# Probabilities of two slots transposed into one tile of two PSUM banks, and one bank for all other transposes

## The chip, the cores and the metric

The kernel runs on one core of one Trainium2 chip. The metric is the device time of one execution in microseconds. Before the change three runs gave a median of 1200.68 us (1199.81 to 1203.39). In the profile PE is TensorE's matmul side and PEld its weight loads, DVE is VectorE, ACT is ScalarE, POOL is GpSimd, SP issues DMAs.

## What is computed

The reference is one layer of a decoder trunk on x of 1 x 1024 x 1024 in float32. The part that matters here is the attention of one block of 128 queries, done for eight blocks, two groups of four heads and two branches (selected keys and a window):

```python
s_s = jnp.einsum('bghqd,bgqkld->bghqkl', qi, kg)
...
p_s = masked_softmax(s_s.reshape(flat_shape),
                     m_s.reshape(bsz, B_KV, 1, Q_BLOCK, k_top * L_SEL)).reshape(s_s.shape)
o_s = jnp.einsum('bghqkl,bgqkld->bghqd', p_s.astype(vg.dtype), vg)
...
s_w = jnp.einsum('bghqd,bgkd->bghqk', qi, kwi)
...
p_w = masked_softmax(s_w, m_w)
o_w = jnp.einsum('bghqk,bgkd->bghqd', p_w.astype(vwi.dtype), vwi)

o = (gi[..., 0:1] * o_c.astype(jnp.float32) + gi[..., 1:2] * o_s.astype(jnp.float32)
     + gi[..., 2:3] * o_w.astype(jnp.float32))
```

Ahead of it stand a norm and the products with w_in (z), beside it the gMLP heads, behind it W_o with a residual, a mixture of 16 experts, a gated projection and a last norm.

## The kernel before

Every float32 product is made of three products of float32r parts: each operand is split into hi (what float32r holds) and lo (the rest), by a copy on ACT and a subtraction on DVE. The kernel runs in stages: z in column chunks (to about 230 us), the attention (239 to 614 us), the last block's way out and the routing (614 to 660), the experts (660 to 1080) and the gated projection (1080 to the end).

The attention takes the query blocks in the order 1, 2, 3, 4, 0, 5, 6, 7. A unit is one block of queries, one group and one branch; a slot is one block of 128 keys of one unit, and there are 132 slots. In slot s the program writes, in this order:

- `trans(s + 1)`: four PE transposes (L643) of the next slot's probabilities P into one PSUM bank `tp`, then the copy `ph` on ACT (L649) and the subtraction `pl` on DVE (L651, written a little later);
- what `later` put off to this slot: the exponentials of a bank of scores one slot after its maxima (L579), then the factors f and the scaling of P by f on POOL (L603), which must be over before that P is transposed;
- the output of a finished unit (L688), and a step of `prep` for a block to come (its queries transposed at L476, scores over the compressed keys S at L482 and L486, their probabilities Pc transposed at L510);
- products that fill (`work`): first of u (L264, 7 in a slot), then of W_o (L770, 3 in a slot), for whose operands `trans4` transposes four tiles (L754);
- one or two banks of scores S (L564, with masks at L566 and L568), followed by their maxima on DVE (L569);
- `mult(s)`: the two products O with ph (L668) and pl (L669); where a unit pair begins, two more with Pc (L662, L663).

The program does not run in that order. A scheduler takes each instruction when its operands and buffers are free by the scheduler's own model of time, earlier written first, and so fixes one order for each engine; the fill has a lower priority (-100000) and may not go ahead of the last transposes written before it. The engines then run their queues strictly in that order, so an instruction at the head of a queue that waits holds up all behind it.

PSUM has eight banks, and in the attention they are: `tp` three (shared in turn by all transposes: L643, L476, L510, L688, L754), S two, O one, and two for the fill. Tiles `ph` and `pl` have three buffers each. `due` holds the slot in which a bank of scores is written at the latest.

Of the kernel before, what the change touches and what calls it, by code (L numbers as in the profile page):

```python
# [34 lines left out]
# columns of the packed constants (shape-only) and of the packed small parameters  # L35
# [8 lines left out]
# columns of w_in, in the order in which they are multiplied  # L44
# [7 lines left out]
class Slots:  # L52
    """Tiles by name from one pool, or in turn from several."""
# [18 lines left out]
class K:  # L72
# [3 lines left out]
    # hi = the part of (src * scale) that float32r holds, lo = the rest of it  # L76
# [41 lines left out]
    # the rotary embedding of z [128, n, 64]  # L118
# [11 lines left out]
    # a chunk of w_in's columns with the norm's gain, hi and lo  # L130
# [16 lines left out]
    # half of two tiles of x, transposed, hi and lo  # L147
# [10 lines left out]
    # the factor of a tile's norm  # L158
# [64 lines left out]
    # the parts of u's way out: each waits for the one before  # L223
    def evac_u(self, tt, p):
# [12 lines left out]
        def two():  # L237
# [3 lines left out]
            # gelu by tanh, whose table holds exp too; the half of it is in what u is multiplied with  # L241
# [16 lines left out]
    # the products of tiles with a chunk, one at a time  # L258
# [38 lines left out]
    def extras(self):  # L297
# [5 lines left out]
        # the mixing weights of the gMLP heads: w_sT[s, h, t] is kept where t >= s  # L303
# [10 lines left out]
    # the gMLP heads mix within chunks of 128 tokens: four tiles of v  # L314
# [18 lines left out]
    # compressed keys (transposed, hi over lo) and values (hi | lo, zero outside their group)  # L333
# [46 lines left out]
    # work that is due some slots on: k slots from now, at the slot's start  # L380
# [10 lines left out]
    # a slot without attention  # L391
# [6 lines left out]
    # Attention of the query blocks in order, a slot being one block of 128 keys of one unit (query  # L398
    # block, group, branch) in the product with the values. A slot holds the scores of units that
    # follow, the transposed probabilities of the next slot, and other products (work).  # L400
    def attention(self, blocks, done, work, count):
# [19 lines left out]
        # where a chunk's probabilities go: the place whose last use is done first  # L421
# [13 lines left out]
        # the heads whose scores share a bank, in order, with the slots in which they are due  # L435
# [5 lines left out]
        for b, (c, _, _) in enumerate(banks):  # L441
            u = chunks[c][0]
            n = len(u["cs"])
            u0 = start[c - chunks[c][1]]
            due.append(u0 - (7 if n == 2 else 5) - (u["banks"][-1] - b))
# [4 lines left out]
        # a bank for scores; what reads the one before it in the same place goes first  # L450
# [6 lines left out]
        # The four heads of a group, transposed: hi over lo, and lo over hi; then the softmax over  # L457
        # the compressed keys of both groups, transposed and split.
        def prep(i):
# [31 lines left out]
            # laid out as [q, head in group, group, key], so that one transpose serves both groups  # L491
# [25 lines left out]
        # The steps of prep: when they are due (before the block's first slot), and which banks and  # L517
        # slots have to come first, as the tiles are those of the block before.
# [23 lines left out]
        # scores of some heads and a chunk; their probabilities follow  # L542
# [43 lines left out]
        # whether the queries for it are ready, or can be  # L586
# [4 lines left out]
        # probabilities times the gate over the sum  # L591
        def stats(u):
# [18 lines left out]
            # the chunks' sums at the maximum of both  # L611
# [17 lines left out]
        # a unit's probabilities, complete  # L629
# [7 lines left out]
        # the probabilities of a block of keys, transposed  # L637
        def trans(s):
            c, u, k, kb = slots[s]
            ensure(u)  # L640
            tp = ps.tile([128, 4, 128], F32, name="tp")
            for h in range(4):
                anchor[0] = PE.transpose(tp[:, h], u["P"][k][:, h, kb * 128:(kb + 1) * 128], self.idf)  # L643
            if kb == u["cs"][k][1] - 1:
                state["transposed"] = c + 1
            ph = sb.tile([128, 512], F32R, name="ph")
            pl = sb.tile([128, 512], F32R, name="pl")
            v = tp.rearrange("p h q -> p (h q)")
            AC.activation(ph, v, AF.Copy)  # L649
            parts[s] = ph, pl  # L650
            return lambda: V.tensor_sub(pl, v, raw(ph))  # L651
# [49 lines left out]
        trans(0)()  # L701
        yield
        for s in range(len(slots)):
            self.now = s
            lo = trans(s + 1) if s + 1 < len(slots) else None
            self.run_later()
            if lo:
                lo()
# [25 lines left out]
    # W_o with the norms' gains: loads (c, columns' half) run ahead of the splits  # L734
# [22 lines left out]
    # 512 columns, transposed, hi and lo  # L757
# [6 lines left out]
    # the products of a half with W_o, one at a time  # L764
# [8 lines left out]
    # The products that fill the slots of the attention: u of the last four tiles, then W_o of the  # L773
    # blocks that are done, the residual, and the experts' input with its router logits.
    def work(self, W, blocks):
# [63 lines left out]
        for n, i in enumerate(blocks[:-1]):  # L839
# [16 lines left out]
            for k in range(2):  # L856
                yield from self.prod(p[k], X["tob"], 1, k, False, True)
                add(X, k, p[k])
                if k == 0:
                    trans_h(X, 0)  # L860
                else:
                    rest(X, N)
        # the last query block's part that doesn't wait for its attention
        X = M[blocks[-1]]
        for k in range(2):
            s = slice(k * 512, (k + 1) * 512)
# [1021 lines left out]
```

## Time and profile before

| | us |
|---|---|
| median of three runs | 1200.68 |
| span of the profiled execution | 1201.4 |
| attention, 239.3 to 614.3 | 375.0 |
| PE busy in the whole span | 1127.4 (94%) |
| DVE, ACT, POOL busy in the span | 772.5, 676.6, 573.0 |

A row of the view of groups gives the line, the engine, the operation with its output and input, how many there are, their busy time and the mean length of one. A matmul's length is not the time that it holds PE for, as matmuls overlap: that is the distance from one start to the next in the timeline. "PEclk" is the granted TensorE clock as a share of the full one (1.00 is 2.4 GHz, 0.50 is 1.2 GHz).

### The profile page before, as it was taken

To read this page: it belongs to the slowest core of one execution; us is meant where nothing else is said; L and a number is where in the kernel's file an instruction comes from. 1 tells how busy PE (TensorE), PEld (TensorE's weight loads), DVE (VectorE), ACT (ScalarE), POOL (GpSimd) and SP (SyncE) were. 2 spreads that over 40 slices of the span, in tenths; PEclk is the share of its full clock that TensorE was granted. 3 is DMA by queue.
4 is the path that set the end of the run, shared out by engine and by line. 5 is a ranking of instruction groups with operands and counts; after the bars stand their busy time and mean duration, and the time that the engine had idled before them with its cause. 6 is when DMAs were issued, how large, how long until landed. Compare 5 with 4: busy or idle time off the path is not lost. (4 is left out here: it accounts for less than half of the span.)

```text
span 1201.4 us, 17857 instructions
## 1 busy us (share of the span) xinstructions
PE 1127.4 (94%) x5993; PEld 866.5 (72%) x5993; DVE 772.5 (64%) x1207; ACT 676.6 (56%) x1306; POOL 573.0 (48%) x639
## 2 busy tenths in 40 slices
PE   7999999899999999999996799999999999959996
PEld 5798778687788888887873566677666766635886
DVE  4461245467876787767649867698657875636764
ACT  6652155467667777666633456667565756435433
POOL 1461342467544343434324776578556865322542
PEclk9999999999899999999998899999999999989999
DMA  8685243412432120231176498997899976465561
GB/s 273 199 215 134 72 127 90 138 58 88 179 105 69 47 97 19 80 115 49 66 280 240 157 340 306 344 370 292 309 320 322 333 251 199 126 249 190 175 220 70
DMA packets 75849, 219.66 MB, mean 183 GB/s; under 512 B 12776, under 2 KB 20328, under 8 KB 71136
## 3 DMA queue, kind: packets, MB, share of 16 engines
q1 hardware_dynamic: 63200, 177.68, 42.9%
q0 software_dynamic: 7792, 27.77, 7.5%
q10 hardware_dynamic: 4752, 12.93, 2.8%
q8 instruction: 52, 0.85, 0.3%
q14 instruction: 53, 0.43, 0.1%
HBM read 247.44 MB, written 40.11 MB: 239 GB/s over the span
## 5 line engine op out<-in xcount | busy, mean ns | idle before, releaser
L1407 DVE TENSOR_TENSOR wl<-ra,wh 128x1024 fp32r<-128x1024 f32 x128 | 218.8, 1727 | 62.1 <-ACT wh L1406 48.3
L1407 POOL TENSOR_TENSOR wl<-ra,wh 128x1024 fp32r<-128x1024 f32 x64 | 171.3, 2678 | 120.2 <-ACT wh L1406 105.0
L1406 ACT ACTIVATE wh<-ra 128x1024 fp32r<-128x1024 f32 x176 | 180.8, 1057 | 77.1 <-PE y L90 44.0
L264 PE MATMUL z<-w,xh 128*128 128x512 f32 (+1 forms) x576 | 170.9, 378 | 7.8 <-ACT w L83 7.5
L603 POOL TENSOR_SCALAR P<-P,f 128x384 f32<-128x384 f32 (+3 forms) x188 | 105.6, 585 | 104.7 <-DVE f L624 61.8
L579 ACT ACTIVATE P<-S,nm 128x256 f32<-128x256 f32 (+3 forms) x192 | 105.5, 556 | 49.3 <-DVE nm L569 45.6
L264 PEld LDWEIGHTS z<-w,xh 128*128 128x128 f32 x576 | 104.9, 190 | 27.1 <-ACT w L83 7.5
L90 PE MATMUL gu<-wh,mxl 128*128 128x512 f32 x272 | 109.3, 402 | 11.2 <-DVE mxl L81 11.2
L89 PE MATMUL gu<-wl,mxh 128*128 128x512 f32 x272 | 109.4, 402 | 8.7 <-DVE wl L1407 7.9
L88 PE MATMUL gu<-wh,mxh 128*128 128x512 f32 x272 | 114.5, 421 | 0.8 <-ACT mxh L80 0.8
L651 DVE TENSOR_TENSOR pl<-tp,ph 128x512 fp32r<-128x512 f32 x132 | 89.8, 685 | 39.0 <-ACT ph L649 38.4
L569 DVE TENSOR_REDUCE nm<-S 128x1 f32<-128x384 f32 (+3 forms) x148 | 91.6, 627 | 31.5 <-PE S L568 18.9
L264 PE MATMUL z<-w,xl 128*128 128x512 f32 (+1 forms) x288 | 108.6, 378 | 1.2 <-DVE xl L81 1.2
L649 ACT ACTIVATE ph<-tp 128x512 fp32r<-128x512 f32 x132 | 78.3, 601 | 42.0 <-PE tp L643 41.4
L564 PE MATMUL S<-kT,qT 128*128 128x384 f32 (+3 forms) x384 | 92.7, 350 | 7.7 <-ACT P L579 5.6
L770 PE MATMUL wo<-wo,th 128*128 128x512 f32 x256 | 90.1, 425 | 0.0
L643 PE MATMUL tp<-c,P 128*128 128x128 f32 x528 | 84.0, 277 | 0.6 <-POOL P L603 0.6
L564 PEld LDWEIGHTS S<-kT,qT 128*128 128x128 f32 x384 | 63.1, 196 | 17.2 <-ACT P L579 7.9
L643 PEld LDWEIGHTS tp<-c,P 128*128 128x128 f32 x528 | 65.7, 143 | 12.6 <-POOL P L603 0.9
L88 PEld LDWEIGHTS gu<-wh,mxh 128*128 128x128 f32 x272 | 52.2, 192 | 23.8 <-ACT wh L1406 7.5
L90 PEld LDWEIGHTS gu<-wh,mxl 128*128 128x128 f32 x272 | 51.9, 191 | 24.0 <-DVE mxl L81 12.1
L89 PEld LDWEIGHTS gu<-wl,mxh 128*128 128x128 f32 x272 | 52.0, 191 | 21.6 <-DVE wl L1407 9.9
(370 smaller groups left out, 2481.2 us busy)
## 6 DMA issues: line engine op xcount, KB each, us to landing
ra<-in_moe_w_gate SPq DMA_DIRECT2D x32, 1024.0 KB
ra<-in_moe_w_up SPq DMA_DIRECT2D x32, 1024.0 KB
ra<-in_moe_w_down SPq DMA_DIRECT2D x32, 1024.0 KB
rq<-in_moe_w_gate SPq DMA_DIRECT2D x40, 512.0 KB
rq<-in_moe_w_up SPq DMA_DIRECT2D x40, 512.0 KB
rq<-in_moe_w_down SPq DMA_DIRECT2D x40, 512.0 KB
y_scr<-yo ACTq DMA_DIRECT2D x19, 512.0 KB
wraw<-in_w_in SPq DMA_DIRECT2D x32, 256.0 KB
```

The source lines that it names most:

```text
L88: mm(out, xh, wh, start=first, stop=False)
L89: mm(out, xh, wl, start=False, stop=False)
L90: mm(out, xl, wh, start=False, stop=last)
L264: self.nc.tensor.matmul(p[:, :n], x, w, start=(cc == 0 and j == 0), stop=(cc == 7 and j == 2))
L564: PE.matmul(S[:, x], qT[i, g][:, h0 + x, a], kk, start=(x + a == 0), stop=(x == hp - 1 and a == 1 and not (dm or wm)))
L569: V.tensor_reduce(u["nm"][:, h0:h0 + hp, k], S, axis=AX.X, op=OP.max, negate=True)
L579: AC.activation(u["P"][k][:, h], S[:, x], AF.Exp, bias=u["nm"][:, h, k:k + 1], accum_out=u["l"][:, h, k:k + 1])
L603: e.tensor_scalar(P, P, f[:, h, k:k + 1], 1.0, op0=OP.mult, op1=OP.mult)
L643: anchor[0] = PE.transpose(tp[:, h], u["P"][k][:, h, kb * 128:(kb + 1) * 128], self.idf)
L770: self.nc.tensor.matmul(p, x, w[:, s], start=first and k + a == 0, stop=last and k == 3 and a == 2)
L1406: AC.activation(hi, w, AF.Copy)
L1407: (G if k in pool else V).tensor_tensor(lo, w, raw(hi), op=OP.subtract)
```

## The change

Where slot s is even, the program transposes the probabilities of slots s + 1 and s + 2 together, eight transposes into a tile `tpp` of two banks, of which there is one; those of the second slot go first. The eight have a high priority (offset 50000). Two copies `ph` and two subtractions `pl` follow. All other transposes share one bank `tp`; two that were in `tp` at the end of the attention and in the routing move to the bank pair of the fill. Banks of scores are due one slot earlier. In the stage of z the three banks `tp` stay (one from one pool, two from a second that is closed ahead of the attention, and whose place S and `tpp` then take). Beside that only comments are taken out. The number of instructions of each kind is the same before and after. Lines from 648 on move: L643, L649, L651, L668, L669, L688, L754 and L770 are L648, L655, L657, L675, L676, L695, L761 and L777 after.

```diff
-            due.append(u0 - (7 if n == 2 else 5) - (u["banks"][-1] - b))
+            due.append(u0 - (8 if n == 2 else 6) - (u["banks"][-1] - b))
...
-        def trans(s):
-            c, u, k, kb = slots[s]
-            ensure(u)
-            tp = ps.tile([128, 4, 128], F32, name="tp")
-            for h in range(4):
-                anchor[0] = PE.transpose(tp[:, h], u["P"][k][:, h, kb * 128:(kb + 1) * 128], self.idf)
-            if kb == u["cs"][k][1] - 1:
-                state["transposed"] = c + 1
-            ph = sb.tile([128, 512], F32R, name="ph")
-            pl = sb.tile([128, 512], F32R, name="pl")
-            v = tp.rearrange("p h q -> p (h q)")
-            AC.activation(ph, v, AF.Copy)
-            parts[s] = ph, pl
-            return lambda: V.tensor_sub(pl, v, raw(ph))
+
+        def trans(ss):
+            for s in ss:
+                ensure(slots[s][1])
+            tps = ps.tile([128, 2, 512], F32, name="tpp")
+            tps = [tps[:, n] for n in range(len(ss))]
+
+            with self.tc.high_priority(offset=50000):
+                for s, v in reversed(list(zip(ss, tps))):
+                    c, u, k, kb = slots[s]
+                    for h in range(4):
+                        anchor[0] = PE.transpose(v[:, h * 128:(h + 1) * 128], u["P"][k][:, h, kb * 128:(kb + 1) * 128], self.idf)
+                    if kb == u["cs"][k][1] - 1:
+                        state["transposed"] = max(state["transposed"], c + 1)
+            los = []
+            for s, v in zip(ss, tps):
+                ph = sb.tile([128, 512], F32R, name="ph")
+                pl = sb.tile([128, 512], F32R, name="pl")
+                AC.activation(ph, v, AF.Copy)
+                parts[s] = ph, pl
+                los.append(lambda pl=pl, v=v, ph=ph: V.tensor_sub(pl, v, raw(ph)))
+            return los
...
-            lo = trans(s + 1) if s + 1 < len(slots) else None
+            los = trans(range(s + 1, min(s + 3, len(slots)))) if s % 2 == 0 else []
             self.run_later()
-            if lo:
+            for lo in los:
                 lo()
...
-            p = ps.tile([128, 512], F32, name="wo", tag=("O", "tp")[n])
+            p = ps.tile([128, 512], F32, name="wo", tag=("O", "fl")[n])
...
-                self.ps = Slots(tp=[(pm, 3)], z=[(pz, 3)])
+                self.ps = Slots(tp=[(pm, 1), (pm2, 2)], z=[(pz, 3)])
...
+                pm2_st.close()
                 pS = pool("pS", space=PSUM)
+                self.ps.add("tp", [(pm, 1)])
+                self.ps.add("tpp", [(pS, 1)])
                 self.ps.add("S", [(pS, 2)])
...
-        pp = ps.tile([128, 512], F32, name="tp")
+        pp = ps.tile([128, 512], F32, name="fl")
...
-        pn = ps.tile([128, 512], F32, name="tp")
+        pn = ps.tile([128, 512], F32, name="fl")
```

What stands in a row on PE moves with it. The first place is an ordinary stretch of the attention on PE with the W_o fill; th and tl are hi and lo of what goes through W_o. Before:

```order
L643 MATMUL tp<-c,P 128x128 x4
L770 MATMUL wo<-wo,th 128x512 x2
L770 MATMUL wo<-wo,tl 128x512
L668 MATMUL O<-ph,V 128x512
L669 MATMUL O<-pl,V 128x512
L643 MATMUL tp<-c,P 128x128 x4
L770 MATMUL wo<-wo,th 128x512 x2
L668 MATMUL O<-ph,V 128x512
L770 MATMUL wo<-wo,tl 128x512
L669 MATMUL O<-pl,V 128x512
L643 MATMUL tp<-c,P 128x128 x4
```

After, on PE, a stretch of the same kind:

```order
L675 MATMUL O<-ph,V 128x512
L676 MATMUL O<-pl,V 128x512
L675 MATMUL O<-ph,V 128x512
L648 MATMUL tpp<-c,P 128x128 x8
L676 MATMUL O<-pl,V 128x512
L777 MATMUL wo<-wo,th 128x512 x2
L777 MATMUL wo<-wo,tl 128x512
L777 MATMUL wo<-wo,th 128x512 x2
L777 MATMUL wo<-wo,tl 128x512
L564 MATMUL S<-kT,qT 128x384 x2
```

Two groups of four, each with three products of the fill behind it, have become one group of eight with six behind it, and the eight stand just ahead of the product with the last `pl` of the pair before.

The second place is the change from the u fill to the W_o fill on PE, where the first blocks' attention is short. Before:

```order
L568 MATMUL S<-mb,idb 128x128
L564 MATMUL S<-kT,qT 128x512 x2
L568 LDWEIGHTS idb
L568 MATMUL S<-mb,idb 128x128
L754 MATMUL tp_3087<-c,oa 128x128 x4
L754 MATMUL tp_3101<-c,ob 128x128
L643 MATMUL tp<-c,P 128x128 x4
L754 MATMUL tp_3101<-c,ob 128x128 x3
L564 MATMUL S<-kT,qT 128x512 x2
```

After, on PE, at the same change of fill:

```order
L564 MATMUL S<-kT,qT 128x512 x2
L568 LDWEIGHTS idb
L568 MATMUL S<-mb,idb 128x128
L675 MATMUL O<-ph,V 128x512
L676 MATMUL O<-pl,V 128x512
L675 MATMUL O<-ph,V 128x512
L648 MATMUL tpp<-c,P 128x128 x8
L676 MATMUL O<-pl,V 128x512
L564 MATMUL S<-kT,qT 128x512 x2
```

Before, six banks of scores stand in a row, then W_o's first transposes (of oa and ob), and only there the next transposes of P; after, two groups of eight and their products O stand between the banks.

The third place is block 0 (four slots) and the start of block 5 on PE. Before:

```order
L643 MATMUL tp<-c,P 128x128 x4
L754 MATMUL tp_4703<-c,h_4179 128x128 x3
L770 MATMUL wo<-wo,th 128x512 x2
L770 MATMUL wo<-wo,tl 128x512
L688 MATMUL tp<-c,oe 128x128 x4
L669 MATMUL O<-pl,V 128x512
L564 MATMUL S<-kT,qT 128x384 x2
L566 LDWEIGHTS idb
L566 MATMUL S<-mb,idb 128x128
L643 MATMUL tp<-c,P 128x128 x4
L770 MATMUL wo<-wo_3060,th 128x512
```

After, on PE, the same banks of scores:

```order
L564 MATMUL S<-kT,qT 128x384 x2
L566 LDWEIGHTS idb
L566 MATMUL S<-mb,idb 128x128
L695 MATMUL tp<-c,oe 128x128 x4
L564 MATMUL S<-kT,qT 128x384 x2
L566 LDWEIGHTS idb
L566 MATMUL S<-mb,idb 128x128
L669 MATMUL O<-pch,Vc 128x512
L670 MATMUL O<-pcl,Vc 128x512
L675 MATMUL O<-ph,V 128x512
L676 MATMUL O<-pl,V 128x512
L695 MATMUL tp<-c,oe 128x128 x4
```

Before, products of W_o lie between the banks; after, from one group of eight to the next there are nine banks of scores and none of the fill.

## Rows read from the trace of the kernel before

**Rows 1.** Windows: stretch, length, busy us of PE, PEld, DVE, ACT, POOL, PEclk, DMA.

```profile
239.30:614.30 375.00, 369.81 (x2286) 306.49 (x2287) 273.23 (x559) 251.00 (x662) 170.65 (x277) 0.99 0.26 85
```

**Rows 2.** Waits of PE: us in total, times, longest; 240 to 615, then 120 to 240.

```profile
PE S L564 <- ACT P L579: 2.4, 5, 0.8
PE S L564 <- DVE Pc L494: 1.5, 1, 1.5
PE tp L510 <- POOL Pc L505: 0.6, 1, 0.6
...
PE O L669 <- DVE pl L651: 0.2, 1, 0.2
...
PE acc L355 <- DMA w1r<-in_cmp_w_v: 1.5, 1, 1.5
```

**Rows 3.** Windows: the change of fill, and two stretches behind it.

```profile
289.60:309.40 19.80, 16.96 (x90) 12.09 (x89) 13.77 (x25) 14.22 (x35) 16.09 (x25) 0.83 0.45 159
309.40:480.00 170.60, 170.60 (x1105) 145.08 (x1105) 130.18 (x273) 120.85 (x326) 71.85 (x124) 1.00 0.24 80
480.00:600.00 120.00, 118.57 (x731) 96.75 (x730) 83.62 (x180) 77.51 (x205) 45.31 (x73) 1.00 0.24 79
```

**Rows 4.** Timeline around groups of four transposes: start, us, engine, line, count.

```profile
445.19 0.60 PE L643 MATMUL tp<-c,P 128*128 128x128 f32 x4
...
446.10 0.39 PE L770 MATMUL wo<-wo,tl 128*128 128x512 f32 x1
...
446.33 0.60 PE L643 MATMUL tp<-c,P 128*128 128x128 f32 x4
```

**Rows 5.** Timeline of PE around a group of eight.

```profile
475.09 1.04 PE L643 MATMUL tp<-c,P 128*128 128x128 f32 x8
...
476.44 0.40 PE L770 MATMUL wo<-wo,tl 128*128 128x512 f32 x1
476.67 0.62 PE L770 MATMUL wo<-wo,th 128*128 128x512 f32 x2
```

**Rows 6.** Timeline of ACT and DVE behind the group of four at 446.33.

```profile
447.02 0.60 ACT L649 ACTIVATE ph<-tp 128x512 fp32r<-128x512 f32 x1 [0.31 <-PE tp L643]
...
447.65 0.69 DVE L651 TENSOR_TENSOR pl<-tp,ph 128x512 fp32r<-128x512 f32 x1 [0.22 <-ACT ph L649]
```

**Rows 7.** Groups by line and shape, 240 to 615: count, busy us, mean ns, idle before.

```profile
L651 DVE TENSOR_TENSOR pl<-tp,ph 128x512 fp32r<-128x512 f32 x131 | 89.1, 685 | 39.0 <-ACT ph L649 38.4
...
L649 ACT ACTIVATE ph<-tp 128x512 fp32r<-128x512 f32 x132 | 78.3, 601 | 42.0 <-PE tp L643 41.4
...
L579 ACT ACTIVATION_READ_ACCUMULATOR P<-S,nm 128x1 f32 x186 | 38.0, 204 | 0.0
...
L579 ACT ACTIVATE P<-S,nm 128x384 f32<-128x384 f32 x64 | 37.1, 581 | 19.5 <-DVE nm L569 17.8 <-DVE l L620 1.1 <-DVE f L624 0.3
...
L579 ACT ACTIVATE P<-S,nm 128x512 f32<-128x512 f32 x48 | 33.0, 690 | 20.0 <-DVE nm L569 18.1 <-DVE lc L502 1.7 <-PE tp L643 0.2
...
L579 ACT ACTIVATE P<-S,nm 128x256 f32<-128x256 f32 x58 | 27.0, 477 | 8.6 <-DVE nm L569 8.5
```

**Rows 8.** Timeline of PE at the change of fill, with what ended its waits.

```profile
296.71 2.06 PE L486 MATMUL S<-kcT,qT 128*128 128x64 f32 x16
...
300.85 0.73 PE L564 MATMUL S<-kT,qT 128*128 128x512 f32 x2 [1.47 <-DVE Pc L494]
...
303.62 1.22 PE L564 MATMUL S<-kT,qT 128*128 128x512 f32 x2 [0.82 <-ACT P L579]
```

**Rows 9.** Timeline of PE: two banks of scores, and what starts behind each.

```profile
447.46 0.65 PE L564 MATMUL S<-kT,qT 128*128 128x256 f32 x4
...
447.99 0.47 PE L668 MATMUL O<-ph,V 128*128 128x512 f32 x1
...
453.07 0.51 PE L564 MATMUL S<-kT,qT 128*128 128x384 f32 x2
...
453.46 0.60 PE L564 MATMUL S<-kT,qT 128*128 128x384 f32 x2
```

More of the change, by code (lines that the diff above doesn't have):

```diff
@@ L700, in attention @@
             self.dq.pop(0)[1]()
-        trans(0)()
+        trans([0])[0]()
         yield
@@ L1010, in mixer @@
             pm = pool("pm", space=PSUM)
+            pm2_st = ExitStack()
+            pm2 = pm2_st.enter_context(make("pm2", space=PSUM))
             blocks = BLOCKS
```

## The prediction

> **What bounds the kernel now.** I read the windows first, then PE's waits, then the timeline around one group of transposes. The change touches the attention, and the stages behind it start when it ends, so I carry its gain or loss to the end one to one. In its 375.0 us PE is busy 369.8, DVE 273.2, ACT 251.0 and POOL 170.7 [rows 1]: PE is the bound, and only 5.2 us of the stage are idle on it. The waits agree: 2.4 us for exponentials that free a bank of scores, 1.5 for Pc, 0.6 for POOL, and the rest small [rows 2]. So what a new order can win is first of all small: the idle 5.2, what PE spends on changes between transposes and products, and what a half clock costs. In the windows the granted clock is 1.00 (2.4 GHz) from 309 to 600, and 0.83 on the mean at the change of fill, 289.6 to 309.4 [rows 3], where PE also idles 19.80 - 16.96 = 2.84 us. What it can lose is larger: DVE and ACT are at 73% and 67% of the stage, and they are now served in bursts.
>
> **Fewer changes between transposes and products.** A group of four costs PE, from its start to the end of two products behind it, 446.10 - 445.19 = 0.91 us [rows 4]; a product alone is 476.67 - 476.44 = 0.23 [rows 5]. So four transposes cost 0.91 - 0.46 = 0.45. A group of eight, which the old order has in places, costs 476.44 - 475.09 - 0.46 = 0.89 [rows 5]. Two groups of four made one of eight save 0.90 - 0.89 = 0.01 us, and for some 65 pairs about **-0.6**. That is what the change wins by itself; no row shows a larger price of a change.
>
> By the Trainium skill (TensorE: Matmul & The Clock Gate, Part 4: PE-mode transpose) transposes don't count as busy for the clock as products do, so eight in a row speak against the change. Here the trace is against any effect: groups of eight stand in the stretch whose clock is 1.00 [rows 3, 5]. I give it nothing in the sum.
>
> **The way out of the two banks.** There is now one tile of two banks where three banks went round. From the start of four transposes to the copy is 447.02 - 446.33 = 0.69 [rows 4, 6]; four more take 0.89 - 0.45 = 0.44, so 1.13. Then two copies of 0.60 on ACT, and two subtractions of 0.69 on DVE, of which the first runs beside the second copy [rows 7]: 1.13 + 0.60 + 2 x 0.69, and 0.03 for each of three handovers (447.62 to 447.65, [rows 6]), is 3.2 us. Only then can the next eight start, since they stand in PE's order just ahead of the product that needs the same `pl`. What covers this is what PE does between two groups of eight. Priced by these rows, the leanest pair holds 0.89 and ten products, 0.89 + 2.3 = 3.2 us: nothing to spare. But of the 65 pairs in the new order, by such prices, 6 hold under 4 us, 26 hold 4 to 5, 23 hold 5 to 6.5 and 10 more. A pair of 4.6 us has 1.4 to spare, which is two exponentials or maxima ahead of the copies (0.69 each on ACT [rows 7]). I take that most pairs don't wait, and 0.12 us each for the 6 lean ones, **+0.7**. The bounds: nothing (the old order waited 0.2 us in all for `pl`, [rows 2]), and one engine's item (0.7 us) in each of the 26 + 6 lean or middling pairs, +22.
>
> **The change of fill.** Before, PE stands at 300.85 for 1.47 us and at 303.62 for 0.82 [rows 8], with six banks of scores in a row, while the clock falls. After, groups of eight and products O lie between. That covers some of it, but the banks still come at the rate of maxima and exponentials, and ACT, DVE and POOL have the same 14.2, 13.8 and 16.1 us of work there [rows 3]. The stretch can't get shorter than POOL's 16.1: at most -3.7. At least nothing: the waits may move by a bank. The clock's share is at most 0.17 x 19.8 = 3.4 us, and whether it falls again is open. I take **-1.5**, a little under half of that, since five banks still follow each other there with only single transposes between them.
>
> **Block 0.** The price of bunching is paid where a block is short. From one group of eight to the next PE now has no fill behind the first six products. Its work: 0.89 + 6 x 0.23 for the group and its fill, 2.0 for the sixteen products with the compressed keys [rows 8], six groups of four at 0.45, four banks of 256 at 0.53 and four of 384 at 0.39 [rows 9], some 0.5 for one of 512, ten products O at 0.23: 2.3 + 2.0 + 2.7 + 2.1 + 1.6 + 0.5 + 2.3 = 13.5 us. ACT has in the same piece eight copies at 0.60, three other passes over 512 columns at about that (an estimate from the same row), and exponentials with a read of 0.20 each: two of 0.69, four of 0.58, eight of 0.48 [rows 7]: 4.8 + 1.8 + 1.8 + 3.1 + 5.4 = 16.9 us. DVE has about as much. So PE is short of work by 3.4 us, less what ACT has done ahead: **+2.5**, between 0.5 (ACT and the two banks run ahead by three items) and 4.5 (they also start late behind the eight).
>
> **Blocks 6 to 7.** The same in small: seven banks of scores come between two groups. ACT has 0.89 + 4 x 0.78 + 4 x 0.68 = 6.7 us of exponentials there [rows 7], PE 0.5 + 4 x 0.39 + 2 x 0.53 = 3.1 for the banks [rows 9] and 4 x 0.23 + 2 x 0.45 = 1.8 for what lies between: short by 1.8. I take **+1.5**, between 0 and 2.5.
>
> **The rest.** At the start the fill of u now stands behind the second unit's first transposes: PE waits for POOL's scaling there, about one item, **+0.5** (0 to 1). In the stage of z the products of compress (L355) come some us earlier in PE's order, against a wait of 1.5 for a DMA there [rows 2]: **-0.3**, between -1 and +0.5. Scores due one slot earlier: the waits that this can remove are the 2.4 us [rows 2], and they are in the terms above. The single bank `tp` for queries, oe, Pc and the fill's operands: each is emptied by a copy and a subtraction or a reduction, 1.3 us by [rows 7], and they rarely follow each other; 0. The two banks moved to the fill's pair in the tail and routing: 0. The moved lines issue no DMA and pass none on SP's queue that anyone waits for.
>
> **Sum.** -0.6 + 0.7 - 1.5 + 2.5 + 1.5 + 0.5 - 0.3 = +2.8 us. The profiled execution's 1201.4 is the span, 0.7 above the median, so I add to the median: 1200.7 + 2.8 = 1203.5.
>
> **Rivals.** *Faster*: the new order covers the change of fill fully and the clock stays up (-3.7, the POOL bound), the switches give their 0.6, and block 0 is covered by what ACT does ahead (+0.5): 1200.7 - 3.8 = 1196.9, and with the start's and compress's terms at their good ends (0 and -1) 1195.9. For it speaks that the waits of today lie just where the new order puts products between; against it, that a piece of 13.5 us of PE work against 16.9 of ACT's stands in the order itself.
>
> *Slower, by the one tile of two banks*: the eight wait at the head of PE's queue until the second `pl` is through, and all of PE's work stands behind them. The price: each pair loses what ACT and DVE are late beyond its spare time. It decides from two items ahead of the copies (1.4 us in a pair of 4.6). At a mean of 0.15 to 0.2 us for 65 pairs it is +10 to +13 over the median: 1211 to 1214. For it speaks that the eight stand at the very place where the tile comes free by the scheduler's model, with no margin in the order; against it, that ACT and DVE are idle a quarter or more of the stage and that copies stand two and two in their queues. Of this the Trainium skill says (Perfetto Trace Analysis, Matmuls) that independent groups should rotate through different PSUM banks, so that the evacuation of one overlaps the next; three banks did that and one tile does not. The old trace agrees in so far as its wait for `pl` was 0.2 us in all.
>
> *Slower by the clock*: PE's short supply at block 0 brings the granted clock down as at the change of fill, another 3.4 us at most [rows 3]: 1203.5 + 3 = 1206.5.
>
> *Nothing*: the terms are all of them smaller than taken, 1200.7.
>
> **How the numbers follow.** A difference of 0.3% (3.6 us) is about what a measurement of this kernel can tell from none; faster is below 1197.1, slower above 1204.3. The forecast, with its small terms as summed, covers 1199 to 1206: 0.47, of which 0.35 lies below 1204.3 and 0.12 above. Faster by the change of fill: 0.25. One tile binds: 0.19. Clock at block 0: 0.06. Nothing: 0.03. So faster 0.25, same 0.35 + 0.03 = 0.38, slower 0.12 + 0.19 + 0.06 = 0.37. The forecast lies within 0.3% of before. The range 1194 to 1213 takes in the faster rival, with a margin for a clock that also stays up at the attention's start, and most of the price of the one tile; some 0.08 is left out below and 0.09 above.
>
> **What would show it.** In the profile after, the attention should be 376 to 380 us long with PE busy about as before. PE's waits should name S for ACT's exponentials at block 0 (near 430 us) and at blocks 6 to 7, 1 to 3 us each, and `tpp` for DVE's `pl` only in the last block. The distance from the start of eight to the copy should be 1.1 us and a pair's way through about 3.2. The 0.83 at the change of fill should rise. Waits of `tpp` for `pl` all along the stage would show the one tile as the bound; a stage of 370 us or less, with the clock at 1.00 from 290 on and no wait at block 0, would show the faster rival. The sum would be wrong most of all if a change between transposes and products costs more than these rows show, or if ACT and DVE run the pairs' copies later than the order suggests.

## The result and the profile after

The changed kernel is slower: a median of 1231.59 us (1224.79 to 1232.78, four runs) beside 1202.04 us before (1199.81 to 1206.91, four runs). The ratio is 1.0226 (95% interval 1.0202 to 1.0250), some 27 us; the two profiled executions, 1231.1 and 1201.4 us, lie 29.7 apart. The prediction was 1203.5 us with a range of 1194 to 1213; the time lies above the range.

The windows of the profile after, by stage: stretch, length, busy us of PE, PEld, DVE, ACT and POOL, PEclk, DMA. The attention, 375.0 us before [rows 1], is the first row; the other rows are the last block's way out, the experts and the gated projection. The single row below is the last block's way out before.

```profile
239.30:642.00 402.70, 384.29 (x2285) 313.29 (x2284) 266.88 (x560) 248.31 (x660) 168.69 (x274) 0.97 0.24 80
642.00:690.00 48.00, 37.66 (x154) 22.73 (x155) 34.21 (x104) 16.39 (x28) 16.36 (x14) 0.89 0.69 266
690.00:1110.00 420.00, 389.77 (x1939) 267.37 (x1937) 291.23 (x240) 246.19 (x295) 255.11 (x125) 0.98 0.78 280
1110.00:1231.00 121.00, 109.95 (x500) 86.04 (x500) 73.20 (x93) 51.98 (x96) 41.41 (x58) 0.95 0.47 163
```

```profile
614.30:660.00 45.70, 34.87 (x148) 21.32 (x147) 33.38 (x103) 16.29 (x28) 15.42 (x14) 0.93 0.74 278
```

The attention is 27.7 us longer, the stretch behind it 2.3 longer (48.0 for 45.7, at a lower clock), the experts and the projection take what they took. In the attention PE idles 18.4 us where it idled 5.2, and it is busy 14.5 us longer with the same matmuls. In part that is the lower clock. In part it may be short gaps: a product is 0.40 us long in the profile and holds PE for 0.23 [rows 5], so a gap of up to 0.17 behind it doesn't count as idle. Finer windows of the same profile show where:

```profile
327.00:345.00 18.00, 15.26 (x74) 11.92 (x73) 11.55 (x21) 10.53 (x28) 8.52 (x13) 0.81 0.11 38
345.00:380.00 35.00, 35.00 (x227) 30.36 (x226) 22.06 (x51) 21.59 (x58) 11.36 (x20) 1.00 0.26 87
380.00:390.00 10.00, 8.69 (x47) 6.93 (x46) 7.10 (x19) 6.51 (x18) 4.61 (x8) 0.83 0.04 14
390.00:432.00 42.00, 41.97 (x284) 36.42 (x282) 25.11 (x55) 27.50 (x83) 15.57 (x33) 1.00 0.22 76
432.00:476.00 44.00, 38.61 (x220) 30.48 (x220) 29.78 (x67) 28.23 (x80) 17.61 (x32) 0.92 0.20 70
476.00:570.00 94.00, 93.65 (x584) 78.12 (x582) 60.70 (x132) 58.86 (x153) 30.46 (x51) 1.00 0.20 68
570.00:585.00 15.00, 12.96 (x68) 10.14 (x66) 11.53 (x31) 10.88 (x33) 8.20 (x11) 0.89 0.09 35
```

Between these places PE is full (35.00 of 35.00, 41.97 of 42.00, 93.65 of 94.00) at a clock of 1.00. In four stretches at ends of blocks it idles 2.7, 1.3, 5.4 and 2.0 us, and the clock falls to 1.2 GHz for part of each, which costs up to (1 - PEclk) times the stretch by an estimate: 3.4, 1.7, 3.5 and 1.7. Together that is 21.7 us. Before, the clock was 1.00 from 309 to 600, but the change of fill had 2.8 us of idle time and up to 3.4 of clock [rows 3]. Less these, the four stretches explain some 15.5 of the 27.7 us; the rest isn't taken apart.

Three more windows of the same profile are needed to judge the terms of the prediction: the change of fill (the last products of u start at 295, the first of W_o at 312), block 0, and the place behind it where block 0 is finished and block 5 begins.

```profile
295.00:312.00 17.00, 14.85 (x91) 10.68 (x90) 12.30 (x24) 12.08 (x29) 9.40 (x14) 1.00 0.49 149
432.00:447.00 15.00, 12.97 (x82) 10.00 (x82) 12.18 (x29) 11.33 (x34) 4.45 (x8) 1.00 0.04 10
461.00:474.00 13.00, 9.83 (x43) 7.28 (x43) 6.40 (x19) 7.67 (x21) 5.24 (x10) 0.74 0.07 28
```

So the clock now stays up at the change of fill and in block 0, and falls behind block 0. PE's waits in the attention after (us in total, times, longest) are spread over many buffers:

```profile
PE S L564 <- ACT P L579: 5.1, 11, 0.8
PE O L676 <- DVE pl L657: 3.3, 4, 1.1
PE O L675 <- ACT ph L655: 3.2, 4, 1.0
PE tp L695 <- DVE f L621: 1.3, 1, 1.3
...
PE tp L476 <- DVE ob L696: 0.8, 1, 0.8
PE tp L476 <- ACT qT L477: 0.7, 2, 0.5
...
PE tpp L648 <- DVE pl L657: 0.2, 1, 0.2
```

The last row is the recorded rival of the one tile of two banks in its plainest form: the eight transposes wait 0.2 us for it in the whole stage. The largest row, PE's waits for exponentials, was 2.4 before [rows 2]; 2.0 of the 5.1 us lie at blocks 6 to 7 and are the idle time there:

```profile
574.84 0.62 PE L564 MATMUL S<-kT,qT 128*128 128x384 f32 x2 [0.57 <-ACT P L579]
...
577.23 0.62 PE L564 MATMUL S<-kT,qT 128*128 128x384 f32 x2 [0.82 <-ACT P L579]
...
579.33 0.96 PE L564 MATMUL S<-kT,qT 128*128 128x256 f32 x4 [0.65 <-ACT P L579]
```

New against [rows 2] are waits for `tp`, of the output (L695) and the queries (L476), and longer waits of the products O for `ph` and `pl`. The timeline of one such place, all engines, shows them as one chain (start, us, engine, line; in brackets the idle time before):

```profile
461.81 0.66 PE L761 MATMUL tp<-c,ob 128*128 128x128 f32 x4
...
462.68 0.60 ACT L80 ACTIVATE th<-tp 128x512 fp32r<-128x512 f32 x1
...
463.95 0.68 DVE L81 TENSOR_TENSOR tl<-tp,th 128x512 fp32r<-128x512 f32 x1
...
464.55 0.15 DVE L621 TENSOR_TENSOR f<-l 128x4 f32<-128x4 f32 x1
...
464.78 0.63 PE L695 MATMUL tp<-c,oe 128*128 128x128 f32 x4 [1.34 <-DVE f L621]
...
465.41 4.51 POOL L603 TENSOR_SCALAR P<-P,f 128x512 f32<-128x512 f32 x8 [7.74 <-PE tp L695]
465.44 0.69 DVE L696 TENSOR_REDUCE ob<-tp 128x256 f32<-128x512 f32 x1
466.19 0.54 PE L476 MATMUL tp<-idr,qs 128*128 128x128 f32 x4 [0.78 <-DVE ob L696]
466.23 0.63 ACT L883 ACTIVATE junk<-ob 128x512 f32<-128x512 f32 x1 [2.95 <-DVE ob L696]
...
466.86 1.06 ACT L655 ACTIVATE ph<-tpp 128x512 fp32r<-128x512 f32 x2
467.49 0.79 PE L675 MATMUL O<-ph,V 128*128 128x512 f32 x1 [0.76 <-ACT ph L655]
467.81 0.60 ACT L477 ACTIVATE qT<-tp 128x512 fp32r<-128x512 f32 x1
...
468.46 0.75 PE L476 MATMUL tp<-idr,qs 128*128 128x128 f32 x4 [0.18 <-ACT qT L477]
...
469.99 1.91 PE L648 MATMUL tpp<-c,P 128*128 128x128 f32 x8
```

Four users of the one bank `tp` follow each other: the fill's operand, the output, and two halves of the queries. Each can start only when the one before has been emptied, by a copy and a subtraction, a reduction, or a copy. The first is subtracted at 463.95 to 464.63, and L695 starts at 464.78; the profile names f (L621), which ended last ahead of it on DVE, but L695 reads nothing of f. The output's reduction ends at 466.13, and L476 starts at 466.19. All of PE's queue stands behind each. On ACT the square `junk` waits for the reduction, and the two copies `ph` stand behind `junk` in ACT's order, so O waits for `ph` in turn. From the product at 467.49 on a matmul takes 0.79 us where the same line has 0.39 at full clock: the clock has gone to half.

The bank isn't alone at this place. The next eight transposes need probabilities that POOL scales from 465.41 to 469.92, and they run at 469.99. The profile puts POOL's start down to L695, so the chain may hold POOL up as well, but the factor f that POOL needs is ready only at 465.31. Without the chain PE might have waited for POOL in its place, unless the scheduler had put fill there. So what the bank is worth is taken from runs, and not from this timeline.

### The profile page after: what moved, and what is told of

Its sections match the earlier page's. It is cut to its first block, busy times and chain, and to the rows that moved or that the text cites. A ratio compares the mean times of both kernels' runs of the same rounds, so it can differ in the third digit from the quotient of the medians.

```text
span 1231.1 us, 17833 instructions
## 1 busy us (share of the span) xinstructions
PE 1145.0 (93%) x5993; PEld 875.1 (71%) x5993; DVE 766.0 (62%) x1207; ACT 674.2 (55%) x1306; POOL 569.7 (46%) x639
## 5 line engine op out<-in xcount | busy, mean ns | idle before, releaser
L603 POOL TENSOR_SCALAR P<-P,f 128x256 f32<-128x256 f32 (+3 forms) x188 | 104.9, 578 | 133.6 <-DVE f L624 86.3
L657 DVE TENSOR_TENSOR pl<-tpp,ph 128x512 fp32r<-128x512 f32 x132 | 84.9, 684 | 61.8 <-ACT ph L655 60.3
L655 ACT ACTIVATE ph<-tpp 128x512 fp32r<-128x512 f32 x132 | 71.8, 598 | 32.3 <-PE tpp L648 26.1
L777 PE MATMUL wo<-wo,th 128*128 128x512 f32 x256 | 84.4, 408 | 0.0
L648 PE MATMUL tpp<-c,P 128*128 128x128 f32 x528 | 76.3, 284 | 1.0 <-POOL P L603 0.6
L648 PEld LDWEIGHTS tpp<-c,P 128*128 128x128 f32 x528 | 63.8, 147 | 10.8 <-issue 3.0
```

Of the source, the lines that this page charges most:

```text
L603: e.tensor_scalar(P, P, f[:, h, k:k + 1], 1.0, op0=OP.mult, op1=OP.mult)
L648: anchor[0] = PE.transpose(v[:, h * 128:(h + 1) * 128], u["P"][k][:, h, kb * 128:(kb + 1) * 128], self.idf)
L657: los.append(lambda pl=pl, v=v, ph=ph: V.tensor_sub(pl, v, raw(ph)))
```

## The experiments

Three theories at first. **A**: the one bank for all other transposes stops PE at the ends of blocks. **B**: eight transposes in a row with high priority do. **C**: the earlier due does. Each run is timed against the kernel before on the same chip; the ratio is to that, with its 95% interval.

| run | edit | ratio | interval |
|---|---|---|---|
| after | the change | 1.0226 | 1.0202 to 1.0250 |
| e_due | before, due 8 and 6 | 1.0070 | 1.0042 to 1.0099 |
| e_places | before, probabilities 2 banks, others 1 | 1.0155 | 1.0119 to 1.0190 |
| e_pairs | before, pairs in the ring of 3, due 8 and 6 | 1.0107 | 1.0061 to 1.0153 |
| a_noprio | change without high priority | 1.0193 | 1.0158 to 1.0227 |
| e_tp2 | before, 2 shared banks | 1.0111 | 1.0085 to 1.0137 |
| e_p1o2 | before, probabilities 1 bank, others 2 | 1.0217 | 1.0185 to 1.0248 |
| a_split | change, pair in two tiles of one bank | 1.0158 | 1.0124 to 1.0192 |
| a_due75 | change, due 7 and 5 | 1.0227 | 1.0189 to 1.0264 |
| a_fl1 | change, fill 1 bank | 1.0231 | 1.0211 to 1.0252 |
| a_fl1tp2 | a_fl1, others 2 banks | 1.0095 | 1.0069 to 1.0122 |
| e_fl1 | before, fill 1 bank | 1.0044 | 1.0021 to 1.0066 |
| b_fl1tp4 | e_fl1, 4 shared banks | 1.0078 | 1.0054 to 1.0103 |
| a_fl1tp2_split | a_fl1tp2, pair in two tiles | 1.0089 | 1.0060 to 1.0117 |
| a_p2o2_due75 | a_fl1tp2_split, due 7 and 5 | 1.0088 | 1.0059 to 1.0117 |
| e_p2o2 | before, the same places, groups of four | 1.0003 | 0.9981 to 1.0026 |
| e_p2o2_due86 | e_p2o2, due 8 and 6 | 1.0037 | 1.0023 to 1.0051 |
| b_due64 | before, due 6 and 4 | 1.0071 | 1.0048 to 1.0094 |
| b_prio | before, high priority | 0.9991 | 0.9972 to 1.0011 |

### The parts of the change, one at a time

The due alone:

```diff
-            due.append(u0 - (7 if n == 2 else 5) - (u["banks"][-1] - b))
+            due.append(u0 - (8 if n == 2 else 6) - (u["banks"][-1] - b))
```

> The kernel before with one edit: banks of scores are due one slot earlier (8 and 6 for 7 and 5). Theory A (the one bank for all other transposes makes the loss) and theory B (eight transposes in a row with high priority make it): as before, 1197 to 1205 us. Theory C (the earlier scores alone crowd ACT and DVE at the ends of blocks): 1210 us or more, with PE's waits for exponentials up from 2.4 us.

It gave 1.0070: not the nothing that A and B expected. Its median of 1210.17 us just reaches C's range, and PE's waits for exponentials are up as C said, from 2.4 us:

```profile
PE S L564 <- ACT P L579: 6.2, 13, 0.9
```

But 0.7% is less than a third of the change's loss, and where other things differ the due costs half of that or nothing (below). The PSUM places alone, with groups of four:

```diff
+                self.ps.add("tp", [(pm, 1)])
+                self.ps.add("tpp", [(pS, 2)])
...
-            tp = ps.tile([128, 4, 128], F32, name="tp")
+            tp = ps.tile([128, 4, 128], F32, name="tpp")
```

> The PSUM places of the change alone: other transposes share one bank, the probabilities' have two banks of their own, taken one at a time, four transposes each, due and priority as before. Theory A: most of the loss is here, 1218 to 1232 us, with PE waiting at the transposes of oe, of queries and of the fill's operands. Theory B: as before, 1198 to 1206 us. Theory C: as before.

1.0155, some two thirds of the loss, without a pair: A. The pairs alone, in the old ring:

```diff
+            tps = [ps.tile([128, 512], F32, name="tp") for _ in ss]
+            with self.tc.high_priority(offset=50000):
+                for s, v in reversed(list(zip(ss, tps))):
```

> The pairs of the change with the places of before: eight transposes in a row with high priority, into two of the three banks that all transposes share; scores due one slot earlier. Theory A: as before, 1197 to 1206 us, with the change of fill and block 0 at waits of 1 to 3 us. Theory B: most of the loss is here, 1218 to 1232 us.

1.0107 and a median of 1217.58 us, outside what A allowed for (1197 to 1206) and at the foot of B's 1218 to 1232: the pairs and the due are not free either. Of the change itself, the priority taken away:

```diff
-            with self.tc.high_priority(offset=50000):
+            if True:
```

> The changed kernel without the high priority of the eight transposes, all else as changed. Theory A: as the changed kernel, 1225 to 1235 us, as the one bank stays. Theory B: a good part is given back, 1205 to 1218 us.

1.0193 (1226.33 us), in A's range and above B's. Its interval overlaps with the change's, so the priority is a small part at most. The earlier due taken back in the change:

```diff
-            due.append(u0 - (8 if n == 2 else 6) - (u["banks"][-1] - b))
+            due.append(u0 - (7 if n == 2 else 5) - (u["banks"][-1] - b))
```

> The changed kernel with scores due as late as before (7 and 5). If the earlier due costs the same here as it did alone (+6 to +8 us): 1221 to 1226 us. If it is needed so that a pair's probabilities are there in time: 1232 us or more, with waits of the pair's transposes for POOL's scaling.

1.0227, as the change, with 1229.45 us between the two expectations: in its company the due is worth nothing either way, and the pairs don't need it.

### How the banks are divided

Two banks shared by all (the lines are against the run of the places alone; the probabilities are in `tp` again), and three banks divided the other way (against the kernel before):

```diff
-                self.ps.add("tp", [(pm, 1)])
-                self.ps.add("tpp", [(pS, 2)])
+                self.ps.add("tp", [(pm, 1), (pS, 1)])
```

> Groups of four and due as before, but all transposes share two banks in turn in the attention, not three (one PSUM bank is left unused). Theory A1 (too few banks altogether for what DVE and ACT take some 1.3 us to empty): slower, 1212 to 1225 us. Theory A2 (the harm is that each kind has its own bank and can't use the other's): near before, 1200 to 1208 us.

```diff
+                self.ps.add("tp", [(pm, 1), (pS, 1)])
+                self.ps.add("tpp", [(pS, 1)])
```

> Groups of four and due as before, three banks, divided the other way: one for the probabilities, two for the other transposes. Theory A (it is the one bank of the other transposes that stops PE): the waits at oe, queries and operands are gone and the time is 1203 to 1212 us. Theory A1 with the division at fault: 1215 to 1240 us, since a group of four now waits for the copy and the subtraction of the group before, 0.69 + 0.60 + 0.69 = 2.0 us a slot against 2.8 us that a slot lasts.

Two shared banks (1.0111) cost less than three divided as 2 and 1 (1.0155) or 1 and 2 (1.0217); the intervals of the first two overlap. So fewer banks cost, and three divided banks do no better than two shared ones, the other way round clearly worse. In this last run A failed: it expected 1203 to 1212 us, and the 1229.54 us lie where the division at fault was expected. The run with one bank for the probabilities shows what the recorded rival looks like when it does happen; PE's longest waits and the attention of that run:

```profile
PE tpp L644 <- DVE pl L652: 13.8, 36, 1.0
```

```profile
239.30:641.00 401.70, 381.18 (x2279) 301.15 (x2278) 270.82 (x559) 250.89 (x657) 168.59 (x273) 1.00 0.24 80
```

There 36 waits for `pl` are spread over the stage. In the change there is one, of 0.2 us. PE is also busy 11.4 us longer than before here, at a clock of 1.00, so such growth need not be the clock's. The next run splits the pair's tile:

```diff
-            tps = ps.tile([128, 2, 512], F32, name="tpp")
-            tps = [tps[:, n] for n in range(len(ss))]
+            tps = [ps.tile([128, 512], F32, name="tpp") for _ in ss]
...
-                self.ps.add("tpp", [(pS, 1)])
+                self.ps.add("tpp", [(pS, 2)])
```

> The changed kernel with the pair in two tiles of one bank each instead of one tile of two: the first bank is free again one subtraction earlier, and a copy waits for its own four transposes alone. The recorded rival (the one tile of two banks binds): 1200 to 1215 us. Theory A (the one bank of the other transposes): 1224 to 1233 us.

1.0158, which fits neither: some 8 us come back, not the whole. That is no more than a small edit can cost by itself (last part of this section), so it isn't shown that the tile makes them. It is then level with groups of four in the same places (1.0155).

### A second bank for the other transposes, inside the change

All eight banks of PSUM are in use, so the fill gives one up: each half of W_o is finished before the next begins, u leaves its bank at once, and one of the routing's sums goes to the bank of O. The first run does that alone, the second gives the bank to `tp` by the last line of this diff:

```diff
-                ev.append(self.evac_u(tt, p))
+                ev.append(self.evac_u(tt, p))
+                ev[-1][0]()
...
-            trans(N, "oa")
-            for k in range(2):
+                if k:
+                    trans(N, "oa")
                 yield from self.prod(p[k], X["tob"], 1, k, False, True)
...
-            self.ps.add("fl", [(pl, 2)])
+            self.ps.add("fl", [(pl, 1)])
...
+            self.ps.add("tp", [(pm, 1), (pl, 1)])
```

> The changed kernel with one PSUM bank for the fill where it has two (each half of W_o is finished before the next begins, u is taken out of its bank at once; one bank is left unused). It is the base of the next run. Both theories: 1228 to 1240 us, as the change with a little less freedom for the fill.

> The run above with the freed bank given to the other transposes, which then have two. Theory A (their single bank makes the loss at the ends of blocks): 1204 to 1216 us, the idle stretches of PE at the ends of blocks gone and the clock at 1.00 there. Theory B (eight in a row and the one tile of two banks make it): within 5 us of the run above.

1.0231 became 1.0095: the second bank gives back 1.4%, some 16 us. The attention and PE's waits for `tp` in the first run, then in the second:

```profile
239.30:642.00 402.70, 382.67 (x2268) 309.93 (x2267) 264.85 (x557) 246.12 (x654) 166.22 (x271) 0.98 0.24 80
...
PE tp L476 <- ACT qT L477: 1.0, 2, 0.5
PE tp L695 <- DVE tl L81: 0.8, 1, 0.8
```

```profile
239.30:624.00 384.70, 370.40 (x2262) 302.09 (x2262) 264.09 (x557) 243.89 (x653) 166.80 (x271) 1.00 0.25 84
...
PE tp L476 <- ACT qT L477: 1.0, 1, 1.0
```

The idle time goes from 20.0 to 14.3 us and the granted clock to 1.00 for the whole stage, which not even the kernel before has [rows 3]. The time and the clock are what A expected. The idle time is not: a good two thirds of it stay, and the waits for `tp` that the profile names fall only from 1.8 to 1.0 us. Of the 18.0 us of the stage 5.7 are idle time and up to 8 (0.02 of 402.7) are clock. So it is shown that the second bank gives these microseconds back, but not by which waits, beyond the chain above. Nor was the same bank given to the probabilities instead, which might have helped as well. Two runs on the fill's bank in the kernel before, the second with the last line of this diff:

```diff
-            self.ps.add("fl", [(pl, 2)])
+            self.ps.add("fl", [(pl, 1)])
...
+            self.ps.add("tp", [(pm, 3), (pl, 1)])
```

> The kernel before with one bank for the fill, one bank left unused: what that bank costs alone. 1200 to 1208 us if the fill's second bank is not needed, 1210 us or more if it is.

> The kernel before with the fill's second bank given to the transposes: four banks in turn for all. If banks for transposes are what the attention is short of, 1194 to 1200 us; if three were enough, as the run with one bank for the fill.

The bank costs 1.0044 there, and a fourth shared bank doesn't bring it back (1.0078): three shared banks were enough.

### What the rest is

The pair's tile split as above, with two banks for the others; and the same places with groups of four, whose `trans` is that of before with its tile in the probabilities' banks:

```diff
-            tp = ps.tile([128, 4, 128], F32, name="tp")
+            tp = ps.tile([128, 4, 128], F32, name="tpp")
...
+                self.ps.add("tpp", [(pS, 2)])
...
+            self.ps.add("tp", [(pm, 1), (pl, 1)])
```

> The changed kernel with one bank for the fill, two for the other transposes, and the pair in two tiles of one bank each. If the one tile of two banks makes the rest of the loss (it was worth 1.0226 - 1.0158 with one bank for the others): 1203 to 1210 us. If eight in a row make it: 1211 to 1218 us as without the split.

> The same PSUM places (probabilities two, others two, fill one), with groups of four, due and priority as before. Pairing costs or wins what lies between this and the run above. If pairing as such costs: 1201 to 1207 us here and 5 us or more above. If it is worth nothing either way: within 4 us of the run above. If pairs save what was predicted: 0.6 us, not to be seen.

The split is now worth nothing (1.0089 after 1.0095), and groups of four in these places are level with the kernel before (1.0003), although one bank fewer serves the fill. So the pairs as they stand cost 0.9% there, with their due and their priority. Two more runs close the square of pairing and due, by the lines on `due` above, in pairs back to 7 and 5, in fours on to 8 and 6:

> Pairs with high priority, two banks for the probabilities in two tiles, two for the others, one for the fill, scores due as before (7 and 5). If the earlier due makes the rest: 1200 to 1207 us. If the pairing makes it: 1210 to 1218 us.

> Groups of four, the same places, scores due one slot earlier (8 and 6). If the earlier due makes the rest: 1209 to 1216 us. If the pairing makes it: 1200 to 1207 us.

Pairs cost 1.0088 and 1.0089 with the later and the earlier due, fours 1.0003 and 1.0037. Part of it shows in windows of the run with pairs and the old due, then of the run with fours, at the change of fill and at block 0:

```profile
300.00:330.00 30.00, 26.60 (x135) 19.05 (x134) 24.61 (x47) 19.51 (x46) 16.98 (x25) 0.89 0.55 183
432.00:446.00 14.00, 11.81 (x66) 9.39 (x66) 11.23 (x27) 10.22 (x31) 8.74 (x15) 0.88 0.19 70
```

```profile
300.00:330.00 30.00, 27.94 (x166) 20.50 (x165) 25.99 (x50) 21.22 (x54) 18.75 (x29) 1.00 0.52 175
424.00:438.00 14.00, 12.73 (x77) 9.78 (x76) 11.96 (x29) 10.82 (x36) 6.15 (x11) 1.00 0.00 0
```

With pairs PE gets fewer matmuls into equal times at both places and the clock falls; with fours it stays. From 270 to 300 it is the other way round, with a clock of 0.94 in the run with fours and 1.00 with pairs. The windows don't hold the same instructions either, so they don't give the 0.9% by place. Last, two edits of the kernel before that ought to do little:

```diff
-            due.append(u0 - (7 if n == 2 else 5) - (u["banks"][-1] - b))
+            due.append(u0 - (6 if n == 2 else 4) - (u["banks"][-1] - b))
```

> The kernel before with scores due one slot later (6 and 4 for 7 and 5), the opposite of the change's edit. If earlier scores crowd the start of the attention, later ones are as before or better, 1196 to 1204 us; if the order of before is simply a good one among many, 1204 to 1215 us in this direction too.

```diff
+            with self.tc.high_priority(offset=50000):
+                for h in range(4):
+                    anchor[0] = PE.transpose(tp[:, h], u["P"][k][:, h, kb * 128:(kb + 1) * 128], self.idf)
```

> The kernel before with the change's high priority given to its groups of four, nothing else. If an early place of the transposes helps where banks are free: 1195 to 1203 us. If any shift of the order costs as the other small edits did: 1204 to 1215 us.

Scores one slot later cost 1.0071, as one slot earlier did (1.0070); the priority alone is not to be told from none. So the order of before is a good one among its neighbours, and an edit that only shifts it can cost 0.7%. The pairs' 0.9% is hardly more, and isn't shown apart from such a shift. No run was clearly faster than the kernel before.

## Why the prediction was wrong

**What bounds the kernel, and that the stages behind follow one to one.** Right: 27.7 us of attention and 2.3 of its tail became the loss, and the experts did the same work in 420 us as before. That there was little to win and more to lose was right too.

**Fewer changes between transposes and products, -0.6.** Right in that it is nothing to speak of. In the profile after a group of eight with one product behind it takes 457.27 - 456.16 = 1.11 us, so the eight cost 0.88 (0.89 in [rows 5]):

```profile
456.16 1.04 PE L648 MATMUL tpp<-c,P 128*128 128x128 f32 x8
...
456.95 0.48 PE L676 MATMUL O<-pl,V 128*128 128x512 f32 x1
...
457.27 0.62 PE L777 MATMUL wo<-wo,th 128*128 128x512 f32 x2
```

The sentence on the transposes and the clock was rightly left out of the sum: eight in a row stand in the 94 us from 476 to 570 at 1.00. In the attention every stretch with a lower clock is one in which PE idles.

**The way out of the two banks, +0.7, and the rival "one tile".** The count of spare time was right for the stage as a whole: PE is full between the ends of blocks. Splitting the tile gave some 8 us as long as the others have one bank (1.0226 to 1.0158), and nothing once they have two (1.0095 to 1.0089). So the tile may matter where the one bank has already made copies late, which isn't shown. The rule of the Trainium skill (Perfetto Trace Analysis, Matmuls) that independent groups should rotate through different banks stood beside this rival; the runs bear it out for the other bank, the one that was left without a second (1.0231 to 1.0095).

**The single bank `tp`, 0.** This is the step that failed. It priced the bank by how long one user's emptying takes (1.3 us) and said that users rarely follow each other. At the ends of blocks they do: the fill's operand, the output and two halves of the queries in 8 us. And a holding is longer than its two passes. For the first user above, 461.81 to 464.63 is 2.8 us: 0.7 are its transposes, 1.3 the two passes, and 0.9 it waits in the queues of ACT and DVE. In the place of 0 the runs showed 1.4% in the change (1.0231 to 1.0095) and 1.5% with groups of four (1.0155 against 1.0003, where the fill has one bank fewer too), 16 to 18 us. Both are about twice what a small edit cost by itself. The three stretches after in which users of `tp` follow each other fit this: 327 to 345, 380 to 390 and 461 to 474, with 2.7, 1.3 and 3.2 us idle and up to 3.4, 1.7 and 3.4 of clock, 15.7 in all, though 1.2 of the idle time in the first of them is named for exponentials.

**The change of fill, -1.5.** Right, and more was won than taken. From 289.6 to 309.4 there had been 2.8 us idle and up to 3.4 of clock [rows 3]; after, from 295 to 312, 2.2 are idle and the clock is 1.00, the rise that the prediction named as a sign. The gain was lost again a block later, from 327 to 345.

**Block 0, +2.5.** Right. From its group of eight to the first of the next are 16.9 us, where the prediction has 13.5 + 2.5 = 16.0:

```profile
428.09 1.04 PE L648 MATMUL tpp<-c,P 128*128 128x128 f32 x8
...
444.97 0.27 PE L648 MATMUL tpp<-c,P 128*128 128x128 f32 x1
```

PE idles 2.0 us from 432 to 447, at a clock of 1.00, so the rival "slower by the clock" didn't come at block 0. What the prediction didn't see is the place behind it, from 461 to 474.

**Blocks 6 to 7, +1.5.** The place, the cause (exponentials) and the 2.0 us of idle time were right, within 0 to 2.5. The up to 1.7 us of clock were left out: a clock that falls had a rival of its own, with a chance of 0.06 and for block 0 alone, and it happened at 338, 385, 467 and 580.

**The earlier due, 0.** Alone it costs 0.7% in the kernel before, where it adds to the waits for exponentials that it was to remove (6.2 us for 2.4); in the change it costs nothing. **The tail, 0**: 2.3 us, at a lower clock; no run took it apart. Nor did one take apart the small terms of the start and of compress, +0.5 and -0.3.

The parts add up to the whole as far as can be told: 1.55% for the places and 1.07% for pairs with the due make 2.6%, the change costs 2.26%, and the intervals of the parts are some 0.4% to either side. With an order fixed by a scheduler each edit gives a new order, and the sum of such terms is good to about 0.7%, twice the bound for "no change" that the prediction used.

## What to carry to other kernels

In this kernel two banks that all kinds of transposes share in turn cost no more (1.0111) than three that were divided between them (1.0155 and 1.0217). Price a single buffer not by its mean use but at the place where its users follow each other, with the queues of the engines that empty it added to each holding. An idle stretch on PE is to be priced with the half clock that can come with it. And where a scheduler fixes the order, run a small neutral edit of the old kernel before reading a meaning into less than one per cent.

## What was not expected of the hardware

In the run with one bank for the probabilities PE waits for `pl` 36 times, and for 13.8 us in all, and the stage loses as much as in the change. Yet from 300 us on its granted clock is 1.00, with 19.3 us of idle time:

```profile
300.00:641.00 341.00, 321.73 (x1934) 252.96 (x1932) 226.07 (x472) 211.10 (x553) 128.42 (x214) 1.00 0.25 82
```

In the change the idle time comes in a few stretches and the clock is 0.97 on the mean, with 0.81 to 0.92 in those stretches. Nearly the same idle time (20.5 and 18.4 us in the attention) was granted two different clocks. The two differ in how it is spread. Which spread brings the clock down can't be read from these runs: the change itself has 2.2 us idle from 295 to 312 and 2.0 from 432 to 447 at a clock of 1.00, and 1.3 from 380 to 390 at 0.83.
